# Up-projection by block products: plain blocks at the start, another order of the products, sums made in place

## The chip, the cores and the metric

The kernel runs on one core of one Trainium2 chip. The metric is the device time of one execution in microseconds (us); the program was run three times, and the median counts. A core has a matrix engine (TensorE, PE in the profile), a vector engine (VectorE, DVE), a scalar engine (ScalarE, ACT), a general one (GpSimd, POOL, hardly used here) and SyncE (SP), which issues nearly all DMA transfers. Each engine runs its own instructions in a fixed order and waits on semaphores for the others. PE writes its results into banks of an accumulator memory (PSUM), which ACT and DVE read.

## The reference

One layer of a bidirectional hybrid encoder (512 tokens, width 2048), followed by the final norm:

```python
h = x + W_out( sig(gA) * P_A(NAtt(xn)) + sig(gB) * P_B(BiGDN(xn)) ),  xn = RMSNorm(x)
h = h + W_down( relu(RMSNorm(h) W_up)^2 )
y = RMSNorm_final(h)
```

The change lies in `RMSNorm(h) W_up`, the up-projection: 2048 to 8192 for 512 tokens, float32.

## The kernel before, in words

Activations stand transposed: features on the 128 partitions, tokens along the row. All matrix products are made in float32 out of two rounded halves: an operand is split into a high part (a cast on ACT, line 94 or 89) and a low part (source minus high part, a subtraction on DVE, line 95 or 90), and each 128x128 weight block takes three matmuls: high weights with high data, high with low, low with high (lines 115 to 117; 912 to 914 in the up-projection).

The stage before is the output projection. It makes the 16 tiles of h, 128x512 each, in the order 0, 8, 1, 9, ... 7, 15. After each, the tile is stored, its squares are summed for the norm (`stat`, whose steps are taken between matmuls by `pump`), it is scaled by the norm's weights (line 868), and its token halves become operands.

The up-projection treats the weights as 32 pairs of row tiles (m0, m0 + 8), each pair as a 2x2 matrix of blocks A11, A12, A21, A22 (128x1024 each), and h as a 2x2 matrix of X11, X12, X21, X22 (1024 features x 256 tokens). It makes the pair's output with seven block products in place of eight: A11 X11, A12 X21, A22 T4, S1 T1, S2 T2, S3 T3 and S4 X22, with the weight sums S1 = A21 + A22, S2 = S1 + A11, S3 = A21 + A11, S4 = S2 + A12 and four sums T1 to T4 of blocks of h. Each product is 8 blocks x 3 = 24 matmuls of 256 columns. The T sums are made per tile into the tiles TR (lines 878 to 881), and after the last tile they are split into operands: 32 fills, in the order T2, T1, T3, T4. Three accumulator banks a, b, c serve a pair; a product may go on adding to a bank that holds another product, and ACT copies a bank out before that where the value alone is needed too.

Before, the order for a pair is A11 (bank a, copied to t1), S2 (b), S1 (c, copied to t5), A12 (added to a), S3 (added to b), S4 (added to c), A22 (added to b); in pair 0 it is A11, S4, A12, S2, S1, S3, A22. The eviction is nine DVE steps of 256 columns. Each engine's order is settled when the program is built: it follows the code, save that instructions that can start earlier may be put ahead of ones that would wait.

Memory: weight blocks A11, A22, A12 go to four load buffers; `wh` and `wl` (high and low blocks) have three each. The pool `sm` (A21 tiles, weight sums, small eviction tiles) lies over the memory of `tr`, which holds the TR tiles, so what goes into it waits until the fills have read them. `hidD` in DRAM takes the result; the down-projection reads it back (`load_hid`).

Of the kernel before, what the change touches and what calls it, by code (L numbers as in the profile page):

```python
# [49 lines left out]
def tile_hybrid_block(  # L50
# [733 lines left out]
    with ExitStack() as p1:  # L784
# [64 lines left out]
        def operand(src, name):
            t = bq.tile([128, T], F32R, tag="B2", name=name) if name.startswith("X11") else big(name)  # L850
            return split(src, t[:, 0:256], t[:, 256:512])

        lo_t, hi_t = slice(0, 256), slice(256, 512)
        XS = {}
        with ExitStack() as p5:
            tr = p5.enter_context(tc.tile_pool(name="tr", bufs=8, side="right", reuse_waits="tile"))
            TR = []
            xs = []
# [24 lines left out]
            tasks.append(stat("h", sq))
            for o, e in (("T2", 1), ("T1", 0), ("T3", 2), ("T4", 3)):
                for j in range(8):
                    XS[o, j] = operand(TR[j][:, e], f"X{o}_{j}")

        with ExitStack() as p6:
            sm = p6.enter_context(tc.tile_pool(name="sm", bufs=1, side="right", reuse_waits="tile"))

            def load_a(src, name):
                raw = sm.tile([128, 1024], F32, tag="a", name=f"raw_{name}", bufs=2)
                nc.sync.dma_start(out=raw, in_=src)
                return raw

            def sums(name, bufs=4):
                return sm.tile([128, 1024], F32, tag="sum", name=name, bufs=bufs)

            def et(name):
                return sm.tile([128, 256], F32, tag="et", name=name, bufs=6)  # L900
# [6 lines left out]
            def product(ps, w, o, first=False):  # L907
                hi, lo = w
                for j in range(8):
                    rh, rl = XS[o, j]  # L910
# [4 lines left out]
                    if j % NPUMP == NPUMP - 1:
                        pump()

            for i in range(32):
# [1 line left out]
                m1 = m0 + 8  # L920
                a11 = load_raw(wup[m0, 0], f"A11_{i}")
                a21 = load_a(wup[m1, 0], f"A21_{i}")
                a22 = load_raw(wup[m1, 1], f"A22_{i}")
                a12 = load_raw(wup[m0, 1], f"A12_{i}")
                s1, s3 = sums(f"S1_{i}"), sums(f"S3_{i}")
                V.tensor_tensor(out=s1, in0=a21, in1=a22, op=ALU.add)
                V.tensor_tensor(out=s3, in0=a21, in1=a11, op=ALU.add)
                a, b, c = (bank()[:, 0:256] for _ in range(3))
                t1, t5, u2 = et(f"t1_{i}"), et(f"t5_{i}"), et(f"u2_{i}")
                r0, r1 = ev(f"ur{m0}"), ev(f"ur{m1}")  # L930
                s2, s4 = sums(f"S2_{i}"), sums(f"S4_{i}")
                product(a, wsplit(a11, f"A11_{i}"), "11", True)
                S_.copy(out=t1, in_=a)
                V.tensor_tensor(out=s2, in0=s1, in1=a11, op=ALU.add)
                if i == 0:
                    V.tensor_tensor(out=s4, in0=s2, in1=a12, op=ALU.add)
                    product(c, wsplit(s4, f"S4_{i}"), "22", True)
                    S_.copy(out=t5, in_=c)
                    product(a, wsplit(a12, f"A12_{i}"), "21")
                product(b, wsplit(s2, f"S2_{i}"), "T2", True)  # L940
                V.tensor_tensor(out=u2, in0=b, in1=t1, op=ALU.add)
                product(c, wsplit(s1, f"S1_{i}"), "T1", i > 0)
                if i == 0:
                    V.tensor_tensor(out=t5, in0=c, in1=t5, op=ALU.subtract)
                else:
                    S_.copy(out=t5, in_=c)
                    product(a, wsplit(a12, f"A12_{i}"), "21")
                V.scalar_tensor_tensor(out=r0[:, lo_t], in0=a, scalar=0.0, in1=rB[:, lo_t], op0=ALU.max, op1=ALU.mult)
                product(b, wsplit(s3, f"S3_{i}"), "T3")
                V.tensor_tensor(out=t5, in0=b, in1=t5, op=ALU.add)  # L950
                V.tensor_tensor(out=t5, in0=t5, in1=t1, op=ALU.add)
                V.scalar_tensor_tensor(out=r1[:, hi_t], in0=t5, scalar=0.0, in1=rB[:, hi_t], op0=ALU.min, op1=ALU.mult)
                if i > 0:
                    V.tensor_tensor(out=s4, in0=s2, in1=a12, op=ALU.add)
                    product(c, wsplit(s4, f"S4_{i}"), "22")
                V.tensor_tensor(out=u2, in0=c, in1=u2, op=ALU.add)
                V.scalar_tensor_tensor(out=r0[:, hi_t], in0=u2, scalar=0.0, in1=rB[:, hi_t], op0=ALU.max, op1=ALU.mult)
# [153 lines left out]
```

## Time and profile before

| what | us |
|---|---|
| three runs | 2926.62 median, 2923.11 to 2926.89 |
| the profiled execution | 2922.42 |
| its span | 2920.6 |
| PE busy in it | 2850.9 (98%) |
| DVE busy | 1723.6 (59%) |
| ACT busy | 1017.2 (35%) |

The span runs from the first to the last instruction that the profile shows. In the rows of the profile an instruction stands as engine, line, operation, what it writes `<-` what it reads, partitions x elements; numbers of buffers are left out of names, so `wh_A` is the high part of any plain block, `wh_S` that of any sum, `XT` any split T operand, `X` any split plain one. The bracket at the end is the engine's idle time before the instruction and who ended it. Matmuls overlap: their starts, not their durations, say how fast PE goes. The up-projection runs from 1526.94 us (first matmul) to the start of the down-projection at about 2200.

### The profile page before, as it was taken

How to read it: one execution, taken by the hardware profiler on the slowest of the kernel's cores; microseconds unless marked ns; L12 is line 12 of the kernel's file. 1: busy time of each engine (PE TensorE's matmuls, PEld its weight loads, DVE VectorE, ACT ScalarE, POOL GpSimd, SP SyncE). 2: the span in 40 equal slices, each digit the busy share in tenths (PEclk: the TensorE clock that was granted, in tenths of full speed). 3: DMA queues.
4: the chain of work that ended last, by engine and by line, in shares of the span. 5: the costliest groups of instructions: out<-in, count | busy, mean ns of one | idle time of the engine just before them, and what ended most of it. 6: DMA issues, size and time to landing. Idle time of an engine off the chain costs nothing.

```text
span 2920.6 us, 39434 instructions
## 1 busy us (share of the span) xinstructions
PE 2850.9 (98%) x15736; PEld 2462.6 (84%) x15736; DVE 1723.6 (59%) x2592; ACT 1017.2 (35%) x1549; POOL 24.8 (1%) x66
## 2 busy tenths in 40 slices
PE   8999999999999999999996999999999999999998
PEld 6778788888788888888886999999997888888887
DVE  6888769744554444444448888888875242332333
ACT  6444322232333333222334444444444231222332
POOL 0000000000000000000000000000000000000000
PEclk9999999999999999999998999999999999999999
DMA  7655663655632323543433334333437343343332
GB/s 230 190 183 187 211 188 121 205 158 176 190 120 92 92 86 121 172 147 116 143 117 116 127 129 139 130 127 131 131 115 262 98 152 101 119 132 95 109 100 87
DMA packets 170874, 412.31 MB, mean 141 GB/s; under 512 B 34369, under 2 KB 46721, under 8 KB 170689
## 3 DMA queue, kind: packets, MB, share of 16 engines
q1 hardware_dynamic: 170016, 407.69, 43.8%
q0 software_dynamic: 672, 2.10, 0.3%
q8 instruction: 123, 2.02, 0.3%
q14 instruction: 63, 0.51, 0.1%
HBM read 350.84 MB, written 58.88 MB: 140 GB/s over the span
## 4 chain that ended last, share of the span: by engine, by line
PE 87%; DMA 6%; DVE 5%; issue 1%; ACT 1%; SPq 0%; DVEq 0%; ACTq 0%
PE ps_b L117 11%; PE ps_b L115 11%; PE ps_b L116 11%; PE ps_mm L115 9%; PE ps_mm L117 9%; PE ps_mm L116 9%; PE ps_b L912 7%; PE ps_b L913 7%; PE ps_b L914 7%; DMA bB<-rowD 1%; DMA Nd<-bB 1%; DVE wl_in L90 1%; DMA kb<-rowD 0%; DMA XQ<-Nd 0%; PE ps_ax L589 0%
## 5 line engine op out<-in xcount | busy, mean ns | idle before, releaser
L115 PE MATMUL ps_mm<-xh,wh_in 128*128 128x512 f32 x1416 | 565.9, 400 | 3.2 <-ACT wh_in L89 3.2
L117 PE MATMUL ps_mm<-xh,wl_in 128*128 128x512 f32 x1416 | 559.0, 395 | 0.7 <-DVE wl_in L90 0.7
L116 PE MATMUL ps_mm<-xl,wh_in 128*128 128x512 f32 x1416 | 558.5, 394 | 0.0
L115 PE MATMUL ps_b<-hih,wh_dn 128*128 128x512 f32 x992 | 386.6, 390 | 1.0 <-ACT hih L94 1.0
L117 PE MATMUL ps_b<-hih,wl_dn 128*128 128x512 f32 x992 | 386.0, 389 | 1.3 <-DVE wl_dn L90 1.3
L116 PE MATMUL ps_b<-hil,wh_dn 128*128 128x512 f32 x992 | 386.4, 390 | 0.0
L89 ACT CAST wh_in<-raw_in 128x1024 fp32r<-128x1024 f32 x177 | 186.0, 1051 | 408.7 <-PE ps_mm L116 331.8
L117 PEld LDWEIGHTS ps_mm<-xh,wl_in 128*128 128x128 f32 x1416 | 267.0, 189 | 60.8 <-DVE wl_in L90 1.6
L115 PEld LDWEIGHTS ps_mm<-xh,wh_in 128*128 128x128 f32 x1416 | 267.1, 189 | 58.4 <-ACT wh_in L89 3.6
L116 PEld LDWEIGHTS ps_mm<-xl,wh_in 128*128 128x128 f32 x1416 | 267.0, 189 | 54.8 <-issue 0.2
L89 ACT CAST wh_dn<-raw_dn 128x1024 fp32r<-128x1024 f32 x124 | 130.8, 1055 | 459.5 <-PE ps_b L116 446.5
L90 DVE TENSOR_TENSOR wl_dn<-raw_dn,wh_dn 128x1024 fp32r<-128x1024 f32 x124 | 151.9, 1225 | 230.3 <-ACT wh_dn L89 230.1
L90 DVE TENSOR_TENSOR wl_in<-raw_in,wh_in 128x1024 fp32r<-128x1024 f32 x177 | 216.0, 1221 | 119.8 <-ACT wh_in L89 110.2
L115 PEld LDWEIGHTS ps_b<-hih,wh_dn 128*128 128x128 f32 x992 | 186.2, 188 | 42.0 <-ACT hih L94 3.4
L116 PEld LDWEIGHTS ps_b<-hil,wh_dn 128*128 128x128 f32 x992 | 186.2, 188 | 40.9 <-DVE hil L95 2.3
L117 PEld LDWEIGHTS ps_b<-hih,wl_dn 128*128 128x128 f32 x992 | 186.2, 188 | 40.1 <-DVE wl_dn L90 2.1
L914 PE MATMUL ps_b<-XT,wl_S 128*128 128x256 f32 x768 | 217.3, 283 | 0.0
L913 PE MATMUL ps_b<-XT,wh_S 128*128 128x256 f32 x768 | 217.3, 283 | 0.0
L912 PE MATMUL ps_b<-XT,wh_S 128*128 128x256 f32 x768 | 217.2, 283 | 0.0
L94 ACT CAST wh_S<-S 128x1024 fp32r<-128x1024 f32 x128 | 134.1, 1048 | 211.7 <-PE ps_b L913 202.1
L95 DVE TENSOR_TENSOR wl_S<-S,wh_S 128x1024 fp32r<-128x1024 f32 x128 | 156.6, 1223 | 31.5 <-ACT wh_S L94 29.0
L983 DVE TENSOR_TENSOR Ha<-ps_b,Ha 128x512 f32<-128x512 f32 x62 | 42.9, 692 | 189.2 <-PE ps_b L117 189.2
(352 smaller groups left out, 5204.5 us busy)
## 6 DMA issues: line engine op xcount, KB each, us to landing
raw_in<-in_win SPq DMA_DIRECT2D x177, 512.0 KB
raw_A<-in_wup SPq DMA_DIRECT2D x128, 512.0 KB
raw_dn<-in_wdn SPq DMA_DIRECT2D x124, 512.0 KB
raw_wo<-in_wout SPq DMA_DIRECT2D x32, 512.0 KB
hidD<-ur SPq DMA_DIRECT2D x64, 256.0 KB
hr<-hidD SPq DMA_DIRECT2D x64, 256.0 KB
gD<-g SPq DMA_DIRECT2D x32, 256.0 KB
raw_pa<-in_wpa SPq DMA_DIRECT2D x16, 512.0 KB
```

The costliest lines, as they stand in the source:

```text
L89: S_.copy(out=hi, in_=raw)
L90: V.tensor_tensor(out=lo, in0=raw, in1=hi.bitcast(F32), op=ALU.subtract)
L94: S_.copy(out=hi, in_=src)
L95: V.tensor_tensor(out=lo, in0=src, in1=hi.bitcast(F32), op=ALU.subtract)
L115: PE.matmul(ps, hi[:, w], rh, start=first and kk == 0, stop=False)
L116: PE.matmul(ps, hi[:, w], rl, start=False, stop=False)
L117: PE.matmul(ps, lo[:, w], rh, start=False, stop=last and kk == 7)
L912: PE.matmul(ps, hi[:, c], rh, start=first and j == 0, stop=False, skip_group_check=True)
L913: PE.matmul(ps, hi[:, c], rl, start=False, stop=False, skip_group_check=True)
L914: PE.matmul(ps, lo[:, c], rh, start=False, stop=j == 7, skip_group_check=True)
L983: V.tensor_tensor(out=H[m], in0=ps, in1=H[m], op=ALU.add)
```

## The change

The products get names: P1 = A11 X11, P2 = A12 X21, Q4 = A22 T4, P5 = S1 T1, P6 = S2 T2, P7 = S3 T3, P3 = S4 X22. Banks: P1, P6 and P7 add up in b, P5 and P3 in c; Q4 and P2 each start afresh in a. The order of a pair is Q4, P5, P1, P6, P7, P3, P2. Copies out of the banks are made after Q4, P5, P1 and P6 (lines 980 to 986); the rest are four DVE adds of 256 columns and two steps of 512 columns. S1 is written over A22, S2 over S1, S4 over S2, S3 over A21, in a pool of seven tiles.

Pairs 0 and 1 go together, product by product in turn, and begin with P1 and P2 of both, whose blocks are plain; their operands are filled with the tiles of h. The eight T4 fills are written ahead of these products, the 24 of T1, T2, T3 behind them. Pairs 30 and 31 also go in turn; pairs 2 to 29 go one by one.

```diff
+            ROLE = {"P1": "11", "P2": "21", "P3": "22", "Q4": "T4", "P5": "T1", "P6": "T2", "P7": "T3"}
+            BANK = {"P1": "b", "P6": "b", "P7": "b", "P5": "c", "P3": "c", "Q4": "a", "P2": "a"}
+            FIRST = {"P1", "P5", "Q4", "P2"}
+            ORDER = ("Q4", "P5", "P1", "P6", "P7", "P3", "P2")
...
+                if q == "Q4":
+                    S_.copy(out=tA[:, 0], in_=ps)
+                elif q == "P5":
+                    S_.copy(out=tB[:, 0], in_=ps)
+                elif q == "P1":
+                    S_.copy(out=tA[:, 1], in_=ps)
+                elif q == "P6":
+                    S_.copy(out=tB[:, 1], in_=ps)
+                elif q == "P7":
+                    add(r1[:, hi_t], ps, tB[:, 0])
+                    add(r1[:, lo_t], ps, tA[:, 0])
+                    V.scalar_tensor_tensor(out=r1, in0=r1, scalar=0.0, in1=rB, op0=ALU.min, op1=ALU.mult)
+                    S_.activation(out=r1, in_=r1, func=AF.Square)
+                elif q == "P3":
+                    add(r0[:, hi_t], ps, tB[:, 1])
...
+                    add(r0[:, lo_t], ps, tA[:, 1])
...
+                V.scalar_tensor_tensor(out=r0, in0=r0, scalar=0.0, in1=rB, op0=ALU.max, op1=ALU.mult)
...
+            first = [up_open(i) for i in range(2)]
+            heads = {}
+            for i, p in enumerate(first):
+                for q in ("P1", "P2"):
+                    heads[i, q] = wsplit(p.a11 if q == "P1" else p.a12, f"{q}_u{i}") if (i, q) in ((0, "P1"), (0, "P2"), (1, "P1")) else None
+            tasks.append(stat("h", sq))
+            for o, j in early_fill[:8]:
+                fill(o, j, tr_src[o, j])
+            for i, p in enumerate(first):
+                for q in ("P1", "P2"):
+                    w = heads[i, q] or wsplit(p.a12, f"{q}_u{i}")
+                    p.ps[BANK[q]] = bank()[:, 0:256]
+                    product(p.ps[BANK[q]], w, ROLE[q], True)
+            for o, j in early_fill[8:]:
+                fill(o, j, tr_src[o, j])
...
+            def a_tile(name):
+                return sm.tile([128, 1024], F32, tag="a", name=name, bufs=7)
...
+            up_group((0, 1), ("P1", "P2", "Q4", "P5", "P6", "P7", "P3"), first)
+            for i in range(2, 30):
+                up_group((i,), ORDER)
+            up_group((30, 31), ORDER)
```

Weight sums and products, and the fills:

```diff
+                j = n // 2
                 if n % 2 == 0:
-                    XS["11", m] = operand(xr[:, lo_t], f"X11_{m}")
+                    x0 = xr
+                    fill("11", j, x0[:, lo_t])
+                    V.tensor_tensor(out=TR["T1"][:, j], in0=x0[:, lo_t], in1=x0[:, hi_t], op=ALU.subtract)
...
+                    fill("21", j, xr[:, lo_t])
+                    V.scalar_tensor_tensor(out=TR["T2"][:, j], in0=TR["T1"][:, j], scalar=-1.0, in1=xr[:, hi_t], op0=ALU.mult, op1=ALU.subtract)
+                    V.scalar_tensor_tensor(out=TR["T4"][:, j], in0=TR["T2"][:, j], scalar=-1.0, in1=xr[:, lo_t], op0=ALU.mult, op1=ALU.subtract)
+                    V.tensor_tensor(out=TR["T3"][:, j], in0=xr[:, hi_t], in1=x0[:, hi_t], op=ALU.subtract)
+                    fill("22", j, xr[:, hi_t])
+            operand_tiles(OPS[3:], "x")
+            early_fill = [(o, j) for o in OPS[3:] for j in range(8)]
...
+                elif q == "P5":
+                    if not p.keep:
+                        add(p.a22, p.a22, p.a21)
+                    w = wsplit(p.a22, f"S1_{nm}")
+                elif q == "P6":
+                    if p.keep:
+                        add(p.a22, p.a22, p.a21)
+                        s2 = sums(f"S2_{nm}")
+                    else:
+                        s2 = p.a22
+                    add(s2, p.a22, p.a11)
+                    p.s2 = s2
+                    w = wsplit(s2, f"S2_{nm}")
+                elif q == "P7":
+                    add(p.a21, p.a21, p.a11)
+                    w = wsplit(p.a21, f"S3_{nm}")
+                else:
+                    add(p.s2, p.s2, p.a12)
+                    w = wsplit(p.s2, f"S4_{nm}")
+                bk = BANK[q]
+                if bk not in p.ps:
+                    p.ps[bk] = bank()[:, 0:256]
+                product(p.ps[bk], w, ROLE[q], q in FIRST)
```

In the order of PE in pair 2, before, the last matmuls of the A11 block (bank 12662) and the first with S2 (bank 12663):

```order
L912 MATMUL ps_b_12662<-X11_7_11968,wh_A11_2_12672 128x256
L913 MATMUL ps_b_12662<-X11_7_11968,wh_A11_2_12672 128x256
L914 MATMUL ps_b_12662<-X11_7_11968,wl_A11_2_12673 128x256
L912 MATMUL ps_b_12663<-XT2_0_12050,wh_S2_2_12702 128x256 [waits Activation_49]
L913 MATMUL ps_b_12663<-XT2_0_12050,wh_S2_2_12702 128x256
L914 MATMUL ps_b_12663<-XT2_0_12050,wl_S2_2_12703 128x256 [waits DVE_49]
L912 MATMUL ps_b_12663<-XT2_1_12053,wh_S2_2_12702 128x256
```

and now, the last of P1 and the first of P6, where the wait on ACT is for the copy `tA_u2` out of bank 12710:

```order
L907 MATMUL ps_b_12710<-X11_x7_10846,wh_A11_u2_12706 128x256
L908 MATMUL ps_b_12710<-X11_x7_10846,wh_A11_u2_12706 128x256
L909 MATMUL ps_b_12710<-X11_x7_10846,wl_A11_u2_12707 128x256
L907 MATMUL ps_b_12710<-XT2_x0_12062,wh_S2_u2_12737 128x256 [waits Activation_49]
L908 MATMUL ps_b_12710<-XT2_x0_12062,wh_S2_u2_12737 128x256
L909 MATMUL ps_b_12710<-XT2_x0_12062,wl_S2_u2_12738 128x256 [waits DVE_49]
L907 MATMUL ps_b_12710<-XT2_x1_12063,wh_S2_u2_12737 128x256
```

The product that adds onto the bank now stands directly behind the one that is copied out of it; before, it went to another bank. Later in the same pair, matmuls of P3 (bank 12680) and then the first of P7, which waits for the copy `tB_u2`:

```order
L907 MATMUL ps_b_12680<-X22_x2_10857,wh_S4_u2_12800 128x256
L908 MATMUL ps_b_12680<-X22_x2_10857,wh_S4_u2_12800 128x256
L909 MATMUL ps_b_12680<-X22_x2_10857,wl_S4_u2_12801 128x256
L907 MATMUL ps_b_12680<-X22_x3_10858,wh_S4_u2_12800 128x256
L908 MATMUL ps_b_12680<-X22_x3_10858,wh_S4_u2_12800 128x256
L907 MATMUL ps_b_12710<-XT3_x0_12070,wh_S3_u2_12767 128x256 [waits Activation_49]
L908 MATMUL ps_b_12710<-XT3_x0_12070,wh_S3_u2_12767 128x256
```

The first 11 matmuls of P3 have moved ahead of P7. ACT in pair 2, now, from the copy of Q4 to that of P6:

```order
L980 COPY tA_u2_12670<-ps_b_12645 128x256 [waits PE_49]
L94 CAST wh_S2_u2_12737<-A22_u2_12637 128x1024 [waits DVE_49,Activation_49]
L94 CAST wh_S3_u2_12767<-A21_u2_12638 128x1024 [waits PE_49,Activation_49]
L982 COPY tB_u2_12671<-ps_b_12680 128x256 [waits PE_49]
L984 COPY tA_u2_12670<-ps_b_12710 128x256 [waits PE_49]
L94 CAST wh_S4_u2_12800<-A22_u2_12637 128x1024 [waits DVE_49,Activation_49]
L94 CAST wh_A12_u2_12829<-raw_A12_u2_12635 128x1024 [waits DMAHW6_49,PE_49,Activation_49]
L986 COPY tB_u2_12671<-ps_b_12710 128x256 [waits PE_49]
```

The copies of P1 and P6 out of bank 12710 are two of four; the cast of A12 stands ahead of the last. DVE at the start of the up-projection, before, from the end of the norm's root (`rsy_h`) on; `dg_h` is what the norm's matmul (line 149) reads:

```order
L126 SCALAR_TENSOR_TENSOR rsu_h_12201<-rsu_h_12201,rsa_h_12198 128x4 [waits DVE_49]
L127 SCALAR_TENSOR_TENSOR rsy_h_12200<-rsu_h_12201,rsy_h_12200 128x4 [waits DVE_49]
L145 TENSOR_TENSOR dg_h_12213<-ident_66,rsy_h_12200 128x512 [waits DVE_49]
L879 SCALAR_TENSOR_TENSOR TR7_12045<-TR7_12045,xr15_11972 128x256 [waits Activation_49]
L95 TENSOR_TENSOR X21_7_12039<-xr15_11972,X21_7_12039 128x256 [waits Activation_49]
L95 TENSOR_TENSOR X22_7_12042<-xr15_11972,X22_7_12042 128x256 [waits Activation_49]
L880 TENSOR_TENSOR TR7_12045<-xr15_11972,xr7_11900 128x256
```

and now, from the last T4 fills on:

```order
L95 TENSOR_TENSOR XT4_x5_12051<-TRT4_10835,XT4_x5_12051 128x256 [waits Activation_49]
L95 TENSOR_TENSOR XT4_x6_12052<-TRT4_10835,XT4_x6_12052 128x256 [waits Activation_49]
L95 TENSOR_TENSOR XT4_x7_12053<-TRT4_10835,XT4_x7_12053 128x256 [waits Activation_49]
L145 TENSOR_TENSOR dg_h_12152<-ident_66,rsy_h_12139 128x512
L95 TENSOR_TENSOR XT1_x0_12054<-TRT1_10836,XT1_x0_12054 128x256 [waits Activation_49]
L95 TENSOR_TENSOR XT1_x1_12055<-TRT1_10836,XT1_x1_12055 128x256 [waits Activation_49]
```

`dg_h` has moved behind the T4 fills. At the end of the remaining fills, now:

```order
L95 TENSOR_TENSOR XT3_x6_12076<-TRT3_10838,XT3_x6_12076 128x256 [waits Activation_49]
L95 TENSOR_TENSOR XT3_x7_12077<-TRT3_10838,XT3_x7_12077 128x256 [waits Activation_49]
L914 TENSOR_TENSOR r0_u0_12309<-ps_b_12166,tA_u0_12307 128x256 [waits PE_49,Activation_49]
L914 TENSOR_TENSOR r0_u1_12314<-ps_b_12222,tA_u1_12312 128x256 [waits PE_49,Activation_49]
L95 TENSOR_TENSOR wl_A22_u0_12320<-A22_u0_12299,wh_A22_u0_12319 128x1024 [waits DMAHW6_49,Activation_49]
L914 TENSOR_TENSOR A22_u0_12299<-A22_u0_12299,A21_u0_12300 128x1024 [waits DMAHW7_49,DVE_49]
```

The evictions of P2 of both pairs and the low half of A22 of pair 0 follow the last T3 fill.

## Rows read from the trace of the kernel before

**Rows 1.** page, engine totals (busy us, share of span, instructions) and the chain that ended last

```profile
PE 2850.9 (98%) x15736; PEld 2462.6 (84%) x15736; DVE 1723.6 (59%) x2592; ACT 1017.2 (35%) x1549; POOL 24.8 (1%) x66
...
PE 87%; DMA 6%; DVE 5%; issue 1%; ACT 1%; SPq 0%; DVEq 0%; ACTq 0%
```

**Rows 2.** busy us by stretch, 1700 to 2100: PE, PEld, DVE, ACT, POOL, granted clock, DMA

```profile
1700.00:2100.00 400.00, 400.00 (x3341) 400.00 (x3341) 332.95 (x398) 180.80 (x219) 0.00 (x0) 1.00 0.40 132
```

**Rows 3.** DVE groups by line, 1700 to 2100: busy us, mean ns, idle before

```profile
L95 DVE TENSOR_TENSOR wl_S<-S,wh_S 128x1024 fp32r<-128x1024 f32 x79 | 96.6, 1223 | 17.7 <-ACT wh_S L94 16.1
...
L934 DVE TENSOR_TENSOR S<-S,raw_A 128x1024 f32<-128x1024 f32 x20 | 24.5, 1225 | 0.7
...
L950 DVE TENSOR_TENSOR t<-ps_b,t 128x256 f32<-128x256 f32 x20 | 8.5, 424 | 12.4 <-PE ps_b L914 12.4
```

**Rows 4.** ACT groups by line, same stretch

```profile
L94 ACT CAST wh_S<-S 128x1024 fp32r<-128x1024 f32 x80 | 83.8, 1048 | 127.1 <-PE ps_b L913 127.1
...
L933 ACT COPY t<-ps_b 128x256 f32<-128x256 f32 x20 | 7.3, 364 | 0.0
```

**Rows 5.** timeline, ACT, copies of a bank in two pairs that follow each other

```profile
1800.82 0.36 ACT L933 COPY t<-ps_b 128x256 f32<-128x256 f32 x1
...
1820.95 0.37 ACT L933 COPY t<-ps_b 128x256 f32<-128x256 f32 x1
```

**Rows 6.** timeline, PE, start of the up-projection

```profile
1531.47 0.28 PE L914 MATMUL ps_b<-X,wl_A 128*128 128x256 f32 x1
1555.35 0.58 PE L912 MATMUL ps_b<-X,wh_S 128*128 128x256 f32 x1 [23.61 <-ACT wh_S L94]
...
1555.95 1.05 PE L149 MATMUL ps_b<-dg_h,ones 128*128 128x512 f32 x1
...
1595.62 0.28 PE L912 MATMUL ps_b<-X,wh_A 128*128 128x256 f32 x1
```

**Rows 7.** timeline, DVE, the same place

```profile
1532.75 0.69 DVE L145 TENSOR_TENSOR dg_h<-ident,rsy_h 128x512 f32<-128x512 f32 x1
...
1535.03 10.81 DVE L95 TENSOR_TENSOR XT<-TR,XT 128x256 fp32r<-128x256 f32 x32
1549.47 1.22 DVE L926 TENSOR_TENSOR S<-raw_A,raw_A 128x1024 f32<-128x1024 f32 x1 [3.62 <-DMA raw_A<-in_wup]
```

**Rows 8.** timeline, ACT, the same place

```profile
1529.94 0.72 ACT L868 ACTIVATE xr<-xr,nlw_s 128x512 f32<-128x512 f32 x1 [1.45 <-DMA hTD<-xr]
...
1533.86 7.75 ACT L94 CAST XT<-TR 128x256 fp32r<-128x256 f32 x25 [0.31 <-DVE TR L879]
```

**Rows 9.** chain that ended last, the same place: start us, us, what

```profile
1545.87 3.48 DMA raw_A<-in_wup
```

**Rows 10.** busy us by stretch, around the pause (columns of Rows 2)

```profile
1545.00:1547.00 2.00, 0.00 (x0) 0.00 (x0) 0.84 (x3) 0.00 (x0) 0.00 (x0) 0.50 0.07 18
1558.00:1559.00 1.00, 1.00 (x7) 1.00 (x6) 1.00 (x2) 0.48 (x1) 0.00 (x0) 0.50 0.43 61
```

**Rows 11.** timeline, PE and ACT, last matmul on a weight block and the waiting cast

```profile
1805.26 0.28 PE L913 MATMUL ps_b<-XT,wh_S 128*128 128x256 f32 x1
...
1805.58 1.05 ACT L94 CAST wh_S<-S 128x1024 fp32r<-128x1024 f32 x1 [1.78 <-PE ps_b L913]
```

**Rows 12.** timeline, a matmul of the down-projection that waits for ACT

```profile
2202.88 0.62 ACT L94 CAST hih<-hr 128x512 fp32r<-128x512 f32 x1 [1.10 <-DMA hr<-hidD]
...
2203.54 0.19 PEld L115 LDWEIGHTS ps_b<-hih,wh_dn 128*128 128x128 f32 x1 [0.72 <-ACT hih L94]
2203.55 0.50 PE L115 MATMUL ps_b<-hih,wh_dn 128*128 128x512 f32 x1 [0.29 <-ACT hih L94]
...
2203.88 0.40 PE L117 MATMUL ps_b<-hih,wl_dn 128*128 128x512 f32 x1
...
2204.12 0.39 PE L115 MATMUL ps_b<-hih,wh_dn 128*128 128x512 f32 x1
```

**Rows 13.** timeline, SP, first loads of the down-projection's operands

```profile
2193.62 0.86 SPq L843 DMA_DIRECT2D hr<-hidD  x2
```

More of the change, by code (lines that the diff above doesn't have):

```diff
@@ L847, in tile_hybrid_block, with operand_tiles, fill @@
         bq = p7.enter_context(tc.tile_pool(name="bq", bufs=8, side="right", reuse_waits="tile"))
[L849 to L851 removed]
         lo_t, hi_t = slice(0, 256), slice(256, 512)
+        OPS = ("11", "21", "22", "T4", "T1", "T2", "T3")
         XS = {}
+        def operand_tiles(names, nm):
+            for o in names:
+                for j in range(8):
+                    if o == "11":
+                        XS[o, j] = bq.tile([128, T], F32R, tag="B2", name=f"X11_{nm}{j}")
+                    else:
+                        XS[o, j] = big(f"X{o}_{nm}{j}")
+        def fill(o, j, src):
+            t = XS[o, j]
+            split(src, t[:, lo_t], t[:, hi_t])
         with ExitStack() as p5:
[L856 to L858 removed]
+            tr = p5.enter_context(tc.tile_pool(name="tr", bufs=1, side="right", reuse_waits="tile"))
+            TR = {o: tr.tile([128, 8, 256], F32, name=f"TR{o}") for o in OPS[3:]}
+            operand_tiles(OPS[:3], "x")
             for n, m in enumerate(m for j in range(8) for m in (j, j + 8)):
@@ L883, in tile_hybrid_block @@
[L883 to L900, printed above, removed]
+                    x0 = xr
@@ L915, in product @@
+                    PE.matmul(ps, hi[:, c], t[:, hi_t], start=False, stop=False, skip_group_check=True)
+                    PE.matmul(ps, lo[:, c], t[:, lo_t], start=False, stop=j == 7, skip_group_check=True)
                     if j % NPUMP == NPUMP - 1:
                         pump()
-            for i in range(32):
-                m0 = i // 8 * 16 + i % 8
[L920 to L944, printed above, removed]
-                else:
[L946 to L957, printed above, removed]
@@ new lines, in tile_hybrid_block, with et, more, up_group @@
+            for o, j in early_fill[8:]:
+                fill(o, j, tr_src[o, j])
+        with ExitStack() as p6:
+            sm = p6.enter_context(tc.tile_pool(name="sm", bufs=1, side="right", reuse_waits="tile"))
+            def a_tile(name):
+                return sm.tile([128, 1024], F32, tag="a", name=name, bufs=7)
+            def et(name):
+                return sm.tile([128, 2, 256], F32, tag="et", name=name, bufs=4)
+            def more(p, s22, s21):
+                p.a22, p.a21 = a_tile(f"A22_{p.nm}"), a_tile(f"A21_{p.nm}")
+                nc.sync.dma_start(out=p.a22, in_=s22)
+                nc.sync.dma_start(out=p.a21, in_=s21)
+            def up_group(idx, order, ps=None):
+                ps = ps or [up_open(i) for i in idx]
+                for i, p in zip(idx, ps):
+                    m0, m1 = up_m(i)
+                    more(p, wup[m1, 1], wup[m1, 0])
+                if order[0] == "P1":
+                    for q in ("P1", "P2"):
+                        for i, p in zip(idx, ps):
+                            up_evac(i, p, q, et)
+                    order = order[2:]
+                for q in order:
+                    for i, p in zip(idx, ps):
+                        run_product(p, q, a_tile)
+                        up_evac(i, p, q, et)
+            up_group((0, 1), ("P1", "P2", "Q4", "P5", "P6", "P7", "P3"), first)
+            for i in range(2, 30):
+                up_group((i,), ORDER)
+            up_group((30, 31), ORDER)
```

65 lines of the change are left out of this document (44 added, 21 removed).

## Prediction

> **What bounds the kernel now.** I read the page first: TensorE (PE) is busy 98% of the span and makes up 87% of the chain that ended last [rows 1]. So the question at each place is whether PE waits there, and for whom. The view of busy time by stretch answers it for the loop over row tile pairs: between 1700 and 2100 us PE is busy 400.00 of 400.00 us at granted clock 1.00, VectorE (DVE) 333, ScalarE (ACT) 181 [rows 2]. There 3341 matmuls take 400 us, 0.120 each; a product is 24 of them, 2.87, and a pair is 7 products, 20.1, which two copies one pair apart confirm: 1800.82 and 1820.95 [rows 5]. In this loop nothing that DVE, ACT or a load does less of can be worth anything.
>
> The timeline of PE shows the one place of the up-projection where it does wait, the start: the last matmul of the first product is issued at 1531.47, the next at 1555.35, held by the cast of the first weight sum [rows 6]. The chain of that stretch and the timeline of DVE say why: 32 operand fills on DVE until 1545.8 [rows 7], then a load of weights that had to wait for the memory under them, 3.48 us [rows 9], then the first sum at 1549.47 [rows 7], the second, the third, a cast. The granted clock there is 0.50, and stays so for some matmuls after the pause [rows 10].
>
> **The start.** Two pairs are 14 products; before, they are done when pair 2 begins, 1595.62 [rows 6]. Afterwards PE has four products (P1 and P2 of pairs 0 and 1) that need plain weight blocks only. I walk through the new order with the durations of before.
> ACT now casts pair 1's A12 block ahead of the scaling of the last h tile; the cast needs a weight buffer which the first product frees near 1531.7, takes 1.05 [rows 4], and so moves the scaling, which ended at 1530.66 [rows 8], to about 1533.4. P2 of pair 0, which would end near 1534.4, waits for its last operand and ends near 1534.6. The next matmul in PE's order is the one for the norm (L149). Its operand dg_h was made at 1532.75 [rows 7]; now DVE makes it behind three sums of h blocks, the last two X fills and eight T4 fills. From 1533.4: cast 0.3, three sums at 0.34, ten fills at 0.336 (10.81 over 32, [rows 7]), dg_h 0.69: about 1538.9. PE waits **4.4 us**. Then the norm's two matmul passes (0.5) and two products: 1545.2, or 1545.8 if part runs at the half clock. On DVE 24 fills follow dg_h, 8.1 us, to 1547.0. The first copy of a bank after that (tA of pair 0) goes into memory that lies under the fills' sources, so it waits for the last fill; behind it in ACT's order stand the other tA copy (0.36 each, [rows 4]) and the cast of A22 (1.05): 1548.9. Q4 of pair 0 waits **3.1**. On DVE two adds stand before the low half of that block (1.22, [rows 3]): another **1.0** at the third matmul. Q4 of pair 1 waits for its low half: **0.9**. From there ten products less stalls: 1548.9 + 28.7 + 1.9 = 1579.5. Gain 1595.6 - 1579.5 = **16.1 us**.
> Bounds: with no wait at all the 14 products would end at 1531.6 + 13 x 2.87 + 0.5 = 1569.4, a gain of 26; with the half clock after each pause as after the long one (0.2 rather than 0.12 per matmul for 3.8 us, [rows 6, 10]; 1.5 each) and the loads of A22 and A21 of pair 1 late by one load [rows 9], 12. I take 16, range 12 to 18, since the waits named are in the order itself.
>
> **The loop, what goes.** Nine eviction steps of 0.42 on DVE become four, with two of double width (0.69, as dg_h's shape in [rows 7]): 3.8 us become 3.1; sums made in place change no count of adds; two more copies of 0.36 go to ACT. All of it lies beside PE, which has no idle time: 0. If DVE were the limit, it would be worth 0.7 per pair.
>
> **The loop, what comes.** Before, PE never adds onto a bank right after the product whose value has to be copied out of it: another product of 2.87 us stands between, and the copy (0.36) hides there. Now P6 adds onto bank b directly behind P1, and ACT must copy P1 out in between. PE stands for: last matmul's issue to ACT's start, 0.32 (1805.26 to 1805.58, [rows 11]); the copy 0.364 [rows 4]; ACT's end to PE's start, 0.05 (2202.88 + 0.62 to 2203.55, [rows 12]); less the 0.12 that would pass anyway: 0.61. A matmul that starts after a wait is followed by the next at 0.33 where the one after comes at 0.24 [rows 12]: 0.1 more. I take **0.72**.
> The Trainium skill speaks against the change here: "Perfetto Trace Analysis", Optimizing Tensor Performance, Matmuls, says that independent groups should take turns between banks so that evacuating one lies beside the next one's matmuls. The loop before, where PE never waits, agrees. Another of its rules would cut the restart: "TensorE: Matmul & The Clock Gate", Part 2, step by step, has weight loads pulled ahead of running matmuls. By it the pause would be 0.61 and the sum 3 us less; the row of the waiting matmul shows its weight load at 2203.54, hardly before it [rows 12].
> P7 follows P6 on the same bank. ACT has a cast of A12 (1.05) ahead of the second copy, and this cast waits for P6 too: 0.32 + 1.05 + 0.36 + 0.05, less 0.12 = 1.66 until P7 may begin. The order puts 11 matmuls of P3 between (9 in every other pair), 1.32 or 1.08: 0.34 or 0.58 short; counting a cast that starts one matmul earlier, as it needs only the high block, 0.24 or 0.48. I take **0.37**. Together 1.09 per pair, and pairs 2 to 29 run so: 28 x 1.09 = **30.5 us**. Pairs 0 and 1, and 30 and 31, alternate, so another pair's product stands between: 0.
> Bounds: P6 alone without restart, 28 x 0.61 = 17; the copy alone, 28 x 0.364 = 10; both pauses at 0.72, 40.
>
> **The end.** The first loads for the down-projection are issued some us before the last product, at 2193.62 [rows 13], and the new order leaves them about there: 0, give or take 2.
>
> **Sum.** 2922.42 (the profiled execution; its span is 2920.6) - 16.1 + 30.5 + 0 = 2936.8. It ran 4.2 below the median, 2926.62, and I forecast for a median: **2941**.
>
> **Rivals.**
> A. The start outweighs (faster or the same). The price per pair decides: at 16.1 / 28 = 0.57 us nothing is won or lost. If PE really stood for the copy alone, 10.2 - 16.1 = -5.9: 2921. If the start's waits vanished as well, 17 - 26 = -9: 2918; with 30.5 - 26, 2931. For it: ACT is idle over half of the time, so the copy can start at once. Against it: both hand-overs, 0.32 and 0.05, are in rows, and PE has nothing else in its order.
> B. DVE takes over the loop (slower still). Its work per pair is seven splits and four adds at 1.22 plus 3.1: 16.5 of 20.1, much of it in a row: the sum for P3 follows the one for P6 in place. If the low half of S4 comes 0.4 late in each pair, 11 more: 2952. For it: DVE 83% busy [rows 2]. Against: a pair gets 1.1 longer, which gives DVE as much.
> C. The start gives only 9, since PE idles and the clock falls, or the late loads of pair 1 hold more: 2948.
> D. Less DVE work makes the loop faster: 0, for PE has no idle time there; I give it no chance of its own.
>
> **Chances.** Forecast 0.71 (own range 2934 to 2947), A 0.13, B 0.06, C 0.10. A's half or more is no difference: this kernel's runs tell about 0.2%, 5.9 us, from no change, 2920.8 to 2932.5. Faster 0.05, same 0.08, slower 0.87. The range reaches into A's upper part, C, and the lower half of B: 2930 to 2951.
>
> **What would show it.** In the profile after: in the middle of the up-projection PE's busy time below 100%, one idle of 0.4 to 0.7 per pair before the first matmul of P6 with the copy L984 as releaser, a smaller one before P7 with L986; a pair period of 21.1 to 21.3 instead of 20.1; at the start no 23.6 us pause but about 4.4 before L149 and 3 to 4 before Q4; pair 2 beginning near 1579. It would be wrong if PE stays at 100% in the loop, if the pair period is under 20.7, or if the largest idle time in the loop is released by DVE.

## The result and the profile after

Median 2942.53 us of four runs (2941.27 to 2943.88) against 2926.72 of four (2923.11 to 2926.89): ratio 1.0057, 95% interval 1.004 to 1.0074 (one run of the kernel before more than in the table ahead). The forecast was 2941, slower.

The page of the profile after, engine totals and the chain that ended last, beside [rows 1]: DVE has 36 us less to do, PE's share is the same. PEld is the loading of weights ahead of each matmul.

```profile
PE 2872.9 (98%) x15736; PEld 2471.8 (84%) x15736; DVE 1687.3 (57%) x2495; ACT 1032.7 (35%) x1613; POOL 24.7 (1%) x66
...
PE 88%; DVE 5%; DMA 5%; ACT 1%; issue 1%; SPq 0%; DVEq 0%; ACTq 0%
```

The loop, busy time by stretch as in [rows 2] (PE, PEld, DVE, ACT, POOL, granted clock, DMA): PE is now busy for 391 us of 400, with 3169 matmuls instead of 3341. DVE did become lighter (295 after 333, a part of it because fewer pairs fit into the 400 us; 315 at the old pace, in e1_turns below), and this did not help.

```profile
1700.00:2100.00 400.00, 391.37 (x3169) 382.37 (x3168) 294.53 (x321) 180.87 (x246) 0.00 (x0) 1.00 0.38 125
```

PE's waits from the first product to the start of the down-projection (who waited for whom, us in all, times, longest): the 23.6 us of [rows 6] are gone; one wait is there 28 times, once for each pair that goes alone.

```profile
PE ps_b L907 <- ACT tA_u L984: 12.9, 28, 0.5
PE ps_b L149 <- DVE dg_h L145: 4.1, 1, 4.1
...
PE ps_b L907 <- ACT wh_A_u L94: 1.4, 1, 1.4
PE ps_b L909 <- DVE wl_A_u L95: 1.3, 2, 0.8
```

Shorter waits do not show there, as one matmul's time in the profile reaches over the start of the next. The weight loads, which are shorter, show two more between 1583 and 2190: P7's for the copy L986 in all 28 pairs, and one for the low half of S4 in 14.

```profile
PEld ps_b L907 <- ACT tB_u L986: 4.9, 28, 0.2
PEld ps_b L909 <- DVE wl_S_u L95: 3.3, 14, 0.2
```

The timeline of that wait, PE and ACT: the last matmul of P1, the copy, the first two of P6. From 1803.92 to 1804.66 is 0.74, where 0.12 is usual; the next comes 0.22 later. Together 0.72 lost.

```profile
1803.92 0.28 PE L909 MATMUL ps_b<-X_x,wl_A_u 128*128 128x256 f32 x1
...
1804.24 0.37 ACT L984 COPY tA_u<-ps_b 128x256 f32<-128x256 f32 x1 [1.25 <-PE ps_b L909]
...
1804.66 0.39 PE L907 MATMUL ps_b<-XT_x,wh_S_u 128*128 128x256 f32 x1 [0.46 <-ACT tA_u L984]
...
1804.88 0.28 PE L908 MATMUL ps_b<-XT_x,wh_S_u 128*128 128x256 f32 x1
```

Three copies L984 of pairs that follow each other: the period is 21.12 and 21.37 in turn, mean 21.245, where [rows 5] gave 20.13.

```profile
1761.75 0.37 ACT L984 COPY tA_u<-ps_b 128x256 f32<-128x256 f32 x1 [1.25 <-PE ps_b L909]
...
1782.87 0.37 ACT L984 COPY tA_u<-ps_b 128x256 f32<-128x256 f32 x1 [1.01 <-PE ps_b L909]
...
1804.24 0.37 ACT L984 COPY tA_u<-ps_b 128x256 f32<-128x256 f32 x1 [1.25 <-PE ps_b L909]
```

The other waits, and what differs between the two kinds of pair, are seen where P3 begins, here in a pair with 9 matmuls of P3 ahead of P7. PE stands 0.19 before the first matmul with the low half of S4 (1786.39 to 1786.70) and 0.14 before P7 (1787.51 to 1787.77), 0.10 more after each: 0.29 and 0.24.

```profile
1783.29 0.39 PE L907 MATMUL ps_b<-XT_x,wh_S_u 128*128 128x256 f32 x1 [0.46 <-ACT tA_u L984]
...
1786.39 0.28 PE L908 MATMUL ps_b<-X_x,wh_S_u 128*128 128x256 f32 x1
1786.40 1.05 ACT L94 CAST wh_A_u<-raw_A_u 128x1024 fp32r<-128x1024 f32 x1 [1.01 <-PE ps_b L908]
...
1786.70 0.38 PE L909 MATMUL ps_b<-X_x,wl_S_u 128*128 128x256 f32 x1
...
1786.92 0.28 PE L907 MATMUL ps_b<-X_x,wh_S_u 128*128 128x256 f32 x1
...
1787.35 0.37 ACT L986 COPY tB_u<-ps_b 128x256 f32<-128x256 f32 x1
...
1787.51 0.28 PE L909 MATMUL ps_b<-X_x,wl_S_u 128*128 128x256 f32 x1
...
1787.77 0.39 PE L907 MATMUL ps_b<-XT_x,wh_S_u 128*128 128x256 f32 x1
...
1787.99 0.28 PE L908 MATMUL ps_b<-XT_x,wh_S_u 128*128 128x256 f32 x1
```

These two are not two prices. P7 begins 4.48 us after the first matmul of P6 here (1783.29 to 1787.77) and 4.47 after it in the next pair (1804.66 above, to 1809.13), where 11 matmuls of P3 stand between and PE stands for S4 by 0.05 only. In both it begins 0.05 after the copy L986 ends (1787.35 + 0.37; 1808.72 + 0.36):

```profile
1808.72 0.36 ACT L986 COPY tB_u<-ps_b 128x256 f32<-128x256 f32 x1
...
1809.13 0.39 PE L907 MATMUL ps_b<-XT_x,wh_S_u 128*128 128x256 f32 x1
```

So the copy sets when P7 begins, and the wait for S4 takes time for which PE would otherwise stand for the copy. What this second pause costs is what the periods leave beside P6's 0.72: 0.27 with 11 matmuls between, 0.52 with 9, in the mean 0.395.

The start, PE: P2 of pair 0 ends, the norm's matmul waits for `dg_h`, Q4 of pair 0 waits twice; pair 2 begins 52.42 us after the first product, where [rows 6] and 1526.94 gave 68.68.

```profile
1530.56 0.28 PE L907 MATMUL ps_b<-X_x,wh_P_u 128*128 128x256 f32 x1
...
1538.21 0.28 PE L909 MATMUL ps_b<-X_x,wl_P_u 128*128 128x256 f32 x1
1542.62 2.08 PE L149 MATMUL ps_b<-dg_h,ones 128*128 128x512 f32 x2 [4.13 <-DVE dg_h L145]
...
1552.29 0.39 PE L907 MATMUL ps_b<-XT_x,wh_A_u 128*128 128x256 f32 x1 [1.36 <-ACT wh_A_u L94]
...
1553.55 0.38 PE L909 MATMUL ps_b<-XT_x,wl_A_u 128*128 128x256 f32 x1 [0.76 <-DVE wl_A_u L95]
...
1582.98 0.28 PE L907 MATMUL ps_b<-XT_x,wh_A_u 128*128 128x256 f32 x1
```

DVE there: eight T4 fills, `dg_h`, 24 fills to 1550.6, beside [rows 7].

```profile
1539.19 2.77 DVE L95 TENSOR_TENSOR XT_x<-TRT,XT_x 128x256 fp32r<-128x256 f32 x8
1541.88 0.69 DVE L145 TENSOR_TENSOR dg_h<-ident,rsy_h 128x512 f32<-128x512 f32 x1
1542.48 8.14 DVE L95 TENSOR_TENSOR XT_x<-TRT,XT_x 128x256 fp32r<-128x256 f32 x24
```

### The profile page after: what moved, and what is told of

The parts are those of the page before. It is cut to its first block, busy times and chain, and to the rows that moved or that the text cites. A ratio compares the mean times of both kernels' runs of the same rounds, so it can differ in the third digit from the quotient of the medians.

```text
span 2940.5 us, 39399 instructions
## 1 busy us (share of the span) xinstructions
PE 2872.9 (98%) x15736; PEld 2471.8 (84%) x15736; DVE 1687.3 (57%) x2495; ACT 1032.7 (35%) x1613; POOL 24.7 (1%) x66
## 4 chain that ended last, share of the span: by engine, by line
PE 88%; DVE 5%; DMA 5%; ACT 1%; issue 1%; SPq 0%; DVEq 0%; ACTq 0%
PE ps_b L115 12%; PE ps_b L116 12%; PE ps_b L117 12%; PE ps_mm L115 9%; PE ps_mm L117 9%; PE ps_mm L116 9%; PE ps_b L907 8%; PE ps_b L909 7%; PE ps_b L908 7%; DVE wl_in L90 1%; DMA bB<-rowD 1%; DMA Nd<-bB 1%; DMA gB<-rowD 1%; DMA kb<-rowD 1%; PE ps_ax L589 0%
## 5 line engine op out<-in xcount | busy, mean ns | idle before, releaser
L907 PE MATMUL ps_b<-XT_x,wh_S_u 128*128 128x256 f32 x768 | 222.9, 290 | 13.0 <-ACT tA_u L984 12.9
L909 PE MATMUL ps_b<-XT_x,wl_S_u 128*128 128x256 f32 x768 | 217.4, 283 | 0.0
L908 PE MATMUL ps_b<-XT_x,wh_S_u 128*128 128x256 f32 x768 | 217.2, 283 | 0.0
L95 DVE TENSOR_TENSOR wl_S_u<-A_u,wh_S_u 128x1024 fp32r<-128x1024 f32 x128 | 156.2, 1223 | 71.8 <-ACT wh_S_u L94 71.6
L94 ACT CAST wh_S_u<-A_u 128x1024 fp32r<-128x1024 f32 x128 | 134.3, 1049 | 144.8 <-DVE A_u L914 129.6
L907 PEld LDWEIGHTS ps_b<-XT_x,wh_S_u 128*128 128x128 f32 x768 | 147.1, 192 | 23.6 <-ACT tA_u L984 18.7
```

Source lines behind the costliest of these rows:

```text
L94: S_.copy(out=hi, in_=src)
L95: V.tensor_tensor(out=lo, in0=src, in1=hi.bitcast(F32), op=ALU.subtract)
L907: PE.matmul(ps, hi[:, c], t[:, lo_t], start=first and j == 0, stop=False, skip_group_check=True)
L908: PE.matmul(ps, hi[:, c], t[:, hi_t], start=False, stop=False, skip_group_check=True)
L909: PE.matmul(ps, lo[:, c], t[:, lo_t], start=False, stop=j == 7, skip_group_check=True)
```

## The experiments

All are compared by the time, and by the length of the up-projection in each trace, from the last matmul of the output projection to the first of the down-projection: 672.7 us before, 687.8 after. The kernel before had medians of 2926.7 to 2931.4 beside the runs, so ratios are read, not differences of medians. In the traces of e2, e4, e7, e8, e9 and e10 the start alone takes 0.6 to 0.7 us longer than in the change, at the same code or nearly so (last section); up-projections that differ by no more are taken as equal.

| kernel | median | ratio to before, 95% | up-projection |
|---|---|---|---|
| the change | 2942.5 | 1.0057 (1.0040 to 1.0074) | 687.8 |
| e1_turns | 2912.7 | 0.9946 (0.9934 to 0.9959) | 656.9 |
| e2_start_alone | 2912.6 | 0.9948 (0.9936 to 0.9961) | 657.1 |
| e3_two_copies | 2948.8 | 1.0065 (1.0050 to 1.0081) | 696.7 |
| e4_by_twos | 2911.8 | 0.9946 (0.9932 to 0.9959) | 657.0 |
| e5_second_wait | 2932.4 | 1.0000 (0.9991 to 1.0009) | 675.3 |
| e6_no_plain_start | 2959.5 | 1.0095 (1.0080 to 1.0110) | 699.8 |
| e7_nine_steps | 2916.6 | 0.9949 (0.9934 to 0.9964) | 657.5 |
| e8_norm_first | 2916.6 | 0.9948 (0.9931 to 0.9964) | 657.6 |
| e9_s4_apart_second_wait | 2920.0 | 0.9965 (0.9956 to 0.9974) | 663.5 |
| e10_s4_apart | 2963.4 | 1.0117 (1.0101 to 1.0134) | 709.1 |

**The wait, taken away and made longer.**

```diff
-            ORDER = ("Q4", "P5", "P1", "P6", "P7", "P3", "P2")
+            ORDER = ("Q4", "P1", "P5", "P6", "P3", "P7", "P2")
```

> The changed kernel with one line altered: the order of a pair is Q4, P1, P5, P6, P3, P7, P2, so that between two products on one bank there is always a product on another (b, c, b, c, b). Copies, sums in place, eviction steps and the start stay. Theory (PE stands while ACT copies a bank out, 1.115 us per pair): the pair period falls from 21.245 to 20.13 us, PE busy all of the time between 1700 and 2100, 28 x 1.115 = 31.2 us less than 2942.5: 2911, that is 15 below the kernel before. Rival (DVE's chain of sums made in place sets the pair): the period stays above 20.5, PE waits for wl or wh of a sum, 2920 to 2943.

Measured: 656.9, 30.9 less than the change (31.2 expected); the kernel is 0.54% faster than the one before. In the loop PE never waits:

```profile
1700.00:2100.00 400.00, 400.00 (x3342) 400.00 (x3341) 314.51 (x339) 193.12 (x260) 0.00 (x0) 1.00 0.39 130
```

The same without touching the order of a pair:

```diff
-            for i in range(2, 30):
-                up_group((i,), ORDER)
-            up_group((30, 31), ORDER)
+            for i in range(2, 32, 2):
+                up_group((i, i + 1), ORDER)
```

> The changed kernel with its own order and banks, but all 32 pairs go two at a time in turn, as pairs 0, 1 and 30, 31 do. Another pair's product then stands between P1 and P6 and between P6 and P7. Theory: waits gone, 2911. Rival (the order matters in some other way, or buffers run short with two pairs open, four load buffers for four plain blocks): 2920 or more, PE waits for weights.

Measured: 657.0, PE busy 400.00 of 400 us. Neither the order as such nor the banks cost anything; a neighbour on the same bank does.

The copy after P1 made twice:

```diff
                 elif q == "P1":
                     S_.copy(out=tA[:, 1], in_=ps)
+                    S_.copy(out=tA[:, 1], in_=ps)
```

> The changed kernel with the copy after P1 made twice, to the same place, one behind the other on ACT. Theory: P6 stands for both, 0.33 to 0.37 more per pair in 28 pairs: 9 to 10.4 us above 2942.5, 2952. Rival (the price is the emptying of PE between two products on a bank, or the hand-over alone, and the copy is beside it): no change, 2942.5.

Measured: 696.7, 8.9 more. The timeline shows P6 behind both copies, its gap 1.14 instead of 0.74:

```profile
1810.11 0.28 PE L909 MATMUL ps_b<-X_x,wl_A_u 128*128 128x256 f32 x1
1810.43 0.37 ACT L984 COPY tA_u<-ps_b 128x256 f32<-128x256 f32 x1 [1.02 <-PE ps_b L909]
...
1810.83 0.37 ACT L985 COPY tA_u<-ps_b 128x256 f32<-128x256 f32 x1
...
1811.25 0.39 PE L907 MATMUL ps_b<-XT_x,wh_S_u 128*128 128x256 f32 x1 [0.86 <-ACT tA_u L985]
```

P6's pause grew by the 0.40 from copy to copy, 11.2 over 28 pairs; but now 11 matmuls of P3 stand ahead of P7 in every pair, so the second pause is 0.23 instead of 0.395, and the period grew by 0.235 only (21.48), 6.6 us. The other 2.3 arose ahead of the first single pair, which begins 54.76 after the first product instead of 52.42: the doubled copies of pairs 0 and 1 stand ahead of the cast of A22, so Q4 of pair 0 begins 0.55 later, and behind its waits of 1.80 and 0.69 PE went on at half the clock:

```profile
1556.00:1558.00 2.00, 2.00 (x11) 2.00 (x11) 1.97 (x3) 1.05 (x1) 0.00 (x0) 0.50 1.01 410
```

The ratio of the times, 1.0065 after 1.0057, does not show the 8.9 us (the intervals overlap); the longer wait stands on the trace.

**The start and the rest.** Pairs 2 to 31 as before, everything at the start as changed:

```diff
-            for i in range(2, 30):
-                up_group((i,), ORDER)
-            up_group((30, 31), ORDER)
+            for i in range(2, 32):
...
+                product(a, wsplit(a11, f"A11_{i}"), "11", True)
+                S_.copy(out=t1, in_=a)
+                V.tensor_tensor(out=s2, in0=s1, in1=a11, op=ALU.add)
+                product(b, wsplit(s2, f"S2_{i}"), "T2", True)
...
```

> The start of the change alone: pairs 0 and 1 as in the changed kernel (plain blocks first, the two in turn), pairs 2 to 31 with the order, the separate sums, the banks and the nine eviction steps of before. Theory: the start gives 16.2 us and the rest of the change nothing but the waits: 2926.7 - 16.2 = 2910.5, the same as e1_turns within 2, pair period 20.13. Rival (fewer eviction steps and sums in place are worth something): this is slower than e1_turns by 0.7 us per pair, 20 us, 2931.

Measured: 657.1, 15.6 less than before, and level with e1_turns. So in place or apart, nine steps or six: no difference where PE is the bound. The step count by itself, in the order of e1_turns:

```diff
...
+                    V.scalar_tensor_tensor(out=r1[:, hi_t], in0=r1[:, hi_t], scalar=0.0, in1=rB[:, hi_t], op0=ALU.min, op1=ALU.mult)
                     add(r1[:, lo_t], ps, tA[:, 0])
-                    V.scalar_tensor_tensor(out=r1, in0=r1, scalar=0.0, in1=rB, op0=ALU.min, op1=ALU.mult)
+                    V.scalar_tensor_tensor(out=r1[:, lo_t], in0=r1[:, lo_t], scalar=0.0, in1=rB[:, lo_t], op0=ALU.min, op1=ALU.mult)
...
```

> e1_turns with the two double-width eviction steps cut into four of 256 columns, as wide as those of before. Theory: 0.3 us more on DVE per pair beside a PE that never waits: nothing, as e1_turns within 2 (2911 to 2913). Rival (DVE's work shows once PE's waits are gone): 30 x 0.3 = 9 us more, 2921.

Measured: 657.5 and a ratio within the interval of e1_turns; the rival's 9 us are excluded by the trace.

Without the plain blocks at the start:

```diff
-            for i, p in enumerate(first):
-                for q in ("P1", "P2"):
-                    w = heads[i, q] or wsplit(p.a12, f"{q}_u{i}")
-                    p.ps[BANK[q]] = bank()[:, 0:256]
-                    product(p.ps[BANK[q]], w, ROLE[q], True)
...
-            up_group((0, 1), ("P1", "P2", "Q4", "P5", "P6", "P7", "P3"), first)
+            up_group((0, 1), ORDER)
```

> The changed kernel without the plain start: pairs 0 and 1 still go in turn, but begin with Q4 as the others do, after all 32 fills; the loop is that of the change. Theory by the trace's durations: after the last matmul of the output projection PE waits about 18.6 us for the fills, Q4 of pair 0 then its low half 1.2, pair 1 another 1: the 14 products end 61 to 62 us after that matmul, where the changed kernel needs 52.4 and the one before 68.7. So 2942.5 + 9 = 2951.5: of the 16.2 us won at the start some 9 are the plain blocks and 7 the absence of a chain of sums and of a late load ahead of the second product. Rival (the plain blocks are all of it): 2958.7; rival (they give nothing since DVE's fills set the end of the start): 2942.5.

Measured: 699.8, 12.1 more than the change (9 expected). The trace, PE:

```profile
1552.14 0.58 PE L907 MATMUL ps_b<-XT_x,wh_A_u 128*128 128x256 f32 x1 [12.95 <-ACT wh_A_u L94]
...
1555.89 0.58 PE L909 MATMUL ps_b<-XT_x,wl_A_u 128*128 128x256 f32 x1 [2.95 <-DVE wl_A_u L95]
```

Pair 2 begins 63.7 us after the output projection's last matmul (1535.63 to 1599.34), where the change needs 52.6: the plain blocks give 11.1 of the 16.3 us. The low half of A22 came near the time expected, 20.3 after that last matmul (19.8 expected); what I had left out is the clock: it was at 0.50 after the pause (1556 to 1560), and from 1555.89 the rest of Q4 took 4.9 us instead of 2.6. So 2.3 of the 11.1 are the slower clock.

The norm first, in the order of e1_turns:

```diff
-            for o, j in early_fill[:8]:
-                fill(o, j, tr_src[o, j])
             for i, p in enumerate(first):
+                if i == 1:
+                    for o, j in early_fill[:8]:
+                        fill(o, j, tr_src[o, j])
```

> e1_turns with the eight T4 fills written behind P1 and P2 of pair 0, so that dg_h for the norm's matmul stands ahead of them on DVE. Theory (32 fills in a row on DVE set the end of the start): the wait of 4.1 us before L149 goes or falls below 1.5, and comes back before Q4 of pair 0, which still needs the last fill; up-projection as in e1_turns, 656.8 within 1, time 2911 to 2913. Rival (the wait before L149 is a loss of its own): 2.7 to 4.1 us less, 2908.

Measured: 657.6. The wait before L149 fell from 4.1 to 1.44 and came back before Q4, 5.52 instead of 1.2. Q4 of pair 0 begins 21.7 us after the first product in both: the fills on DVE set it, not the norm.

```profile
1544.77 1.13 PE L149 MATMUL ps_b<-dg_h,ones 128*128 128x512 f32 x2 [1.44 <-DVE dg_h L145]
...
1557.13 0.58 PE L907 MATMUL ps_b<-XT_x,wh_A_u 128*128 128x256 f32 x1 [5.52 <-ACT wh_A_u L94]
...
1558.39 0.58 PE L909 MATMUL ps_b<-XT_x,wl_A_u 128*128 128x256 f32 x1 [0.46 <-DVE wl_A_u L95]
```

**The second wait.** Here the number came out right and the reason wrong.

```diff
-            ORDER = ("Q4", "P5", "P1", "P6", "P7", "P3", "P2")
+            ORDER = ("Q4", "P1", "P5", "P6", "P7", "P3", "P2")
```

> The changed kernel with the order Q4, P1, P5, P6, P7, P3, P2: P5 stands between P1 and P6, so the first wait is gone; P7 still follows P6 on bank b, with 10 or 6 matmuls of P3 put between in turn (11 or 9 in the changed kernel). Theory: P7 may begin 1.57 us after P6's last matmul (hand-over, a cast of 1.05 that stands ahead on ACT, the copy), so the pairs lose 1.57 - 1.20 = 0.37 and 1.57 - 0.72 = 0.85 in turn, mean 0.61: pair period 20.74, 2911 + 28 x 0.61 = 2928, no difference from the kernel before. Rival (the second wait is small whatever stands between, as in the changed kernel, 0.39 per pair): 2922; rival (P6's place was all of it): 2911.

Measured: 675.3, ratio 1.0000, pair periods 20.59 and 21.01. These are losses of 0.46 and 0.88, near the 0.37 and 0.85; but the trace names no copy. The copy L986 ends 0.2 before P7 in both kinds of pair; PE waited at the first matmul with the low half of S4, and DVE shows why: the low halves of S2 and S3 in one row of 2.50, then the sum S4 that goes over S2, a cast, the low half of S4.

```profile
1801.64 2.50 DVE L95 TENSOR_TENSOR wl_S_u<-A_u,wh_S_u 128x1024 fp32r<-128x1024 f32 x2 [1.17 <-ACT wh_S_u L94]
...
1804.06 1.22 DVE L914 TENSOR_TENSOR A_u<-A_u,raw_A_u 128x1024 f32<-128x1024 f32 x1
...
1805.36 1.05 ACT L94 CAST wh_S_u<-A_u 128x1024 fp32r<-128x1024 f32 x1 [0.56 <-DVE A_u L914]
...
1806.44 1.22 DVE L95 TENSOR_TENSOR wl_S_u<-A_u,wh_S_u 128x1024 fp32r<-128x1024 f32 x1 [1.17 <-ACT wh_S_u L94]
...
1807.72 0.38 PE L909 MATMUL ps_b<-X_x,wl_S_u 128*128 128x256 f32 x1 [0.21 <-DVE wl_S_u L95]
```

With S4 in a tile of its own, in the order of e5_second_wait:

```diff
-                    add(p.s2, p.s2, p.a12)
-                    w = wsplit(p.s2, f"S4_{nm}")
+                    s4 = sums(f"S4_{nm}")
+                    add(s4, p.s2, p.a12)
+                    w = wsplit(s4, f"S4_{nm}")
```

> e5_second_wait with S4 written to a tile of its own instead of over S2; in the order of DVE its sum now stands ahead of the low halves of S2 and S3, and 11 or 9 matmuls of P3 stand between P6 and P7. Theory after e5 (there PE stood for the low half of S4, which comes late because S4 may not be written over S2 before S2's low half is made): that wait goes, and what shows is P7's wait for the copy after P6: 1.57 - 1.32 = 0.25 and 1.57 - 1.08 = 0.49 in turn, mean 0.37: pair period 20.50, up-projection 656.8 + 28 x 0.37 = 667 instead of 675.3. Rival (the sum in place has nothing to do with it): period 20.80 as in e5, released by DVE.

Measured: 663.5, period 20.35 (two copies L985, below), and PE's only wait in the loop is for the copy after P6: 0.22 in each pair. The order has 11 matmuls between in every pair, not 11 and 9 as I had read it, so 0.25 was to be expected. The edit is worth 12 us to e5. It took the wait for S4 away, as the theory has it; but it also put 11 matmuls of P3 ahead of P7 where e5 had 10 and 6, and the two are not told apart.

```profile
1798.72 0.37 ACT L985 COPY tA_u<-ps_b 128x256 f32<-128x256 f32 x1
...
1819.07 0.36 ACT L985 COPY tA_u<-ps_b 128x256 f32<-128x256 f32 x1
```

The same edit in the changed kernel alone:

> The changed kernel with S4 in a tile of its own and nothing else. Two matmuls of P3 now stand between P1 and P6, and 11 between P6 and P7 in every pair. Theory: P6's pause 0.72 less 0.24 = 0.48, P7's 0.25, none for the low half of S4: 0.73 per pair instead of 1.115, pair period 20.86, up-projection 687.8 - 28 x 0.385 = 677, about 11 us less than the changed kernel. Rival (as forecast: sums in place are worth nothing either way): 21.24, no difference.

Measured: 709.1, 21 more, against theory and rival. The two matmuls of P3 that now stand ahead of P6 wait for the cast of S4. That cast seems to wait for the weight buffer which P1's last matmuls free: three `wh` buffers go round, so S4's is that of P1's A11, and the last high matmul of P1 is issued at 1814.08, the cast starts at 1814.44, PE goes on at 1815.54. The profile puts that wait down to ACT's own cast before, which had ended 0.89 earlier, so this step is read from code and times and not shown. I had counted the two matmuls as cover and not looked at what they wait for. The period is 21.99, a loss of 1.86 per pair: 1.32 here in place of P6's 0.72, 0.23 before P7, and 0.29 that is new, at the low half of S1 in P5. The first of these in the 18 pairs from 1700 to 2100:

```profile
PE ps_b L907 <- ACT wh_S_u L94: 19.1, 18, 1.1
```

## Why the prediction was right, and where not

Measured in the profiled execution of each kernel:

| step | forecast | measured | from |
|---|---|---|---|
| start, 14 products | -16.1 | -16.3 | 68.68 to 52.42 |
| wait before L149 | 4.4 | 4.13 | timeline |
| Q4 of pair 0, high and low half | 3.1 and 1.0 | 1.36 and 0.76 | timeline |
| pair 0 to pair 1, low half | 0.9 | 0.5 | waits, 1.3 less 0.76 |
| per pair, 28 pairs | +1.09, 30.5 | +1.115, 31.2 | period 20.13 to 21.245 |
| of it P6 | 0.72 | 0.72 | timeline; e1, e3, e4 |
| of it P7 | 0.37 | 0.27 or 0.52, mean 0.395 | periods less 0.72 |
| eviction steps, in-place sums beside PE | 0 | 0 | e2, e7 |
| end | 0 | +0.1 | 603.8 to 635.1, less 31.2 |

The mechanism was right: PE stands while ACT copies a bank, and this outweighs the start. Of the 19.9 us between the spans (2920.6, 2940.5) 15.1 are the up-projection's; 3.6 arose before it (the first product at 1530.56, not 1526.94), ahead of the output projection, where the code is the same, which fits the 4.2 by which the profiled execution of before lay below its median; 1.2 arose behind it.

Some terms were mis-sized. Q4's wait was smaller than forecast and the end of the start the same: PE came later to it, as the two products ahead ran partly at half clock, and Q4's time is set by the last fill, not by PE (e8). The second pause came out at 0.395 for 0.37, partly by luck: without the restart, which I had left out there, it is 0.17 or 0.42 where I had 0.24 or 0.48, and the 0.10 of the restart makes up for that. And rival B's wait was there: PE stood for the low half of S4 in every other pair (0.29 with the restart). It had no price of its own, since P7 begins at the same time after P6 in the pairs with it and in those without; this is read from the start times, as no run takes that wait away and leaves 9 matmuls between. In e5, where the low half of S4 comes later, it was the wait that counted.

Rival A needed a price under 0.57 per pair; it was 1.115. The Trainium skill, "Perfetto Trace Analysis", Optimizing Tensor Performance, Matmuls, whose rule on banks spoke against the change, is borne out with a number: 31 us for 28 pairs, given back whole as soon as a product on another bank stands between (e1, e4). The rule of the Trainium skill that weight loads are pulled ahead ("TensorE: Matmul & The Clock Gate", Part 2, Step-by-step) did not shorten this pause: the matmul after the wait was followed by the next at 0.22, not 0.12, in all 28 pairs.

## What to carry to other kernels

Where an engine is busy all of the time, a change is worth what it does to that engine's waits: 36 us less work on VectorE bought nothing, and a copy of 0.37 us that had lain beside a product cost 0.72 in each pair once the next product wanted its bank. Ask of every accumulation onto a bank that is copied out which product stands between, and of every matmul that is put between what it waits for itself (e10). The start and the loop of one change should be priced and tried apart: the start alone (e2) is 0.5% faster than the kernel before and, by the two ratios, 1.1% faster than the change; e1 and e4 get as far with the loop changed too.
